# A four-layer trunk on one core: the small TensorE steps of an attention head, gathered in one place per head

## The chip, the cores and the metric

The kernel runs on one core of one Trainium2 chip. Its time is the device time of one execution in microseconds (us); three runs of the kernel before gave a median of 1296.69 us. Engines are named as in the profile: PE is TensorE, PEld its weight loads, DVE VectorE, ACT ScalarE, POOL GpSimd, SP SyncE. "L857" is line 857 of the kernel before. Behind the point where the diff takes away a line, the changed kernel's numbers are one lower; the lines that are named here are the same in both.

## The reference, cut to what matters

A trunk of four layers works on 256 tokens of 1024 channels. Each layer has a mixer, a feed-forward block and a gated side input, with two layer norms. Layers 0 and 3 mix by differential attention, layer 1 by a gated recurrence, layer 2 by local attention with a window of 128 tokens and a sink. The change touches the two kinds of attention:

```python
# differential attention (8 heads, each with two score maps)
s = einsum('bmqd,bmkd->bmqk', q, k);  s = where(rel >= 0, s + bias, -inf)
a = softmax(s);  a = a[:, :, 0] - lam_full * a[:, :, 1]
o = einsum('bhqk,bhkv->bhqv', a, v);  o = rms_norm(o, subln) * (1 - lam_init);  return o @ w_out

# local attention (16 query heads that share 2 key heads, with a sink)
m = maximum(max(s), sink);  e = exp(s - m);  a = e / (sum(e) + exp(sink - m))
o = einsum('bnhgqk,bnkhd->bnqhgd', a, v);  return o @ w_out
```

All is float32.

## The kernel before, in words

**Large matmuls.** Weights come from HBM as 1 MB chunks (SP issues them, in the order of use). ScalarE rounds each chunk to a high part `wh` (L124), VectorE subtracts it to get a low part `wl` (L125), and TensorE adds up three products: high by high, high by low, low by high. L177 to L179 are these three where tokens are the rows of the result (feed-forward, V, output projection); L197 and L198 are the same work where channels are the rows (Q and K projection, 16 matmuls per 128 columns), which ScalarE and VectorE then join from two halves (L204, L208).

**Small steps of a head.** In both kinds of attention a head goes through these steps, and "head" in local attention means a pair of query heads, 0 to 7, one for each key head:

- `soft`: scores on TensorE (L644 and L648; in local attention L816 and L818), bias and maximum on VectorE (L653; L821, then the small L830 and L831), exponentials on ScalarE (L661; L836 and, for the sink, L840), normalisation on VectorE (in local attention L841, L842 and the scaling L845 of `e`; in differential attention L673 subtracts the second map).
- `attT`: transposes of `e` on TensorE (three L684; in local attention six L857), copied by ScalarE to `aT` (L686; two L859).
- `pv`: P times V on TensorE (L694 to L696; L868 to L870). In local attention its result is split at once into `hT` (ScalarE L124, VectorE L125), the input of the output projection; in differential attention an RMS norm follows.
- `outT` (differential attention only): transposes of the normed output (L721), then the same split.

**Order.** Large matmuls are pushed to a queue as generators. `self.fill(us)` takes from it about as many as that many microseconds hold, and `self.fill_to(g)` all up to g. The program's text so says where the small steps stand between them. When the program is built, a scheduler sets each engine's order once: it may take an instruction of later text ahead where it counts the earlier one as not ready, if its inputs and its buffer are there. On the chip each engine then works through its own order and waits where an input is not ready.

**PSUM.** The program uses eight banks: four buffers of the tag `mm` (`self.mm_ps()`) and four of the tag `acc` (`self.acc_ps()`). Projections accumulate in `mm`; scores, PV and, before the change, the transposes of local attention use `acc`. Buffers are given in the order of the text.

**Around the change.** In differential attention the loop over 8 heads runs while the Q and K projections of later heads and the second half of V fill the queue. Before, one turn of the loop is: projections up to this head, 2.93 us of filler, `soft(hd)`, `attT(hd-1)`, 2.6 us of filler, `outT(hd-2)`, `pv(hd-1)`; the later heads' `pv` and `outT` stand behind the loop, among the output projection. In local attention a turn is: Q projection up to this head (every second turn), 1.3 us of filler, `soft(a)`, 3.25 us of filler, `pv(a-2)`, 0.65 us of filler, `attT(a-1)`. The Q projection holds less filler than the eight turns ask for. Behind the loop the first parts of the output projection are pushed (`out_part`), with `pv(6)`, `attT(7)` and `pv(7)` among them; each takes two `mm` buffers when it starts.

## Time and profile before

| | us |
|---|---|
| median of three runs (lowest to highest) | 1296.69 (1296.45 to 1298.39) |
| the profiled execution | 1296.76 |
| its span | 1294.8 |
| span, head 0's scores to head 3's scores in local attention | 21.27 (705.80 to 727.07) |
| span, head 3's scores to PV of head 6 | 18.40 (727.07 to 745.47) |

A row of the timeline gives the start in us from the span's beginning, how long the instruction took, the engine, the line, the operation, the tiles out<-in with the shape, and a count where rows of equal instructions are merged; brackets at the end give idle time of the engine just before, and what ended it. A matmul of scores or PV stands in the trace as two rows. Matmuls overlap in these times, the next starting before the one before has ended; so what a matmul costs is read from one start to the next. In a table by stretches the numbers are the stretch, its length, the busy time of PE, PEld, DVE, ACT and POOL, the granted clock of TensorE, the share of the DMA engines, and GB/s.

### The profile page before, as it was taken

To read this page: it belongs to the slowest core of one execution; us is meant where nothing else is said; L and a number is where in the kernel's file an instruction comes from. 1 tells how busy PE (TensorE), PEld (TensorE's weight loads), DVE (VectorE), ACT (ScalarE), POOL (GpSimd) and SP (SyncE) were. 2 spreads that over 40 slices of the span, in tenths; PEclk is the share of its full clock that TensorE was granted. 3 is DMA by queue.
4 is the path that set the end of the run, shared out by engine and by line. 5 is a ranking of instruction groups with operands and counts; after the bars stand their busy time and mean duration, and the time that the engine had idled before them with its cause. 6 is when DMAs were issued, how large, how long until landed. Compare 5 with 4: busy or idle time off the path is not lost.

```text
span 1294.8 us, 18557 instructions
## 1 busy us (share of the span) xinstructions
PE 1287.8 (99%) x7034; PEld 1087.3 (84%) x7034; DVE 937.3 (72%) x1741; ACT 692.0 (53%) x1296; POOL 35.9 (3%) x48
## 2 busy tenths in 40 slices
PE   9999999999999999999999999999999999999998
PEld 6888888888888888888888788888888888888887
DVE  5888766667889877666677796666687877766666
ACT  5885544444754455444537755444447775444443
POOL 0001000000000010000000000000000010000000
PEclk9999999999999999999999999999999999999999
DMA  8745655553733256555547145655538344655540
GB/s 274 289 171 195 230 193 195 184 189 122 267 127 131 77 211 225 185 190 194 195 166 264 66 166 221 202 191 195 195 131 298 131 171 163 234 191 194 195 162 33
DMA packets 43081, 240.09 MB, mean 185 GB/s; under 512 B 4512, under 2 KB 11744, under 8 KB 16496
## 3 DMA queue, kind: packets, MB, share of 16 engines
q1 hardware_dynamic: 42992, 238.91, 52.8%
q8 instruction: 55, 0.90, 0.3%
q14 instruction: 34, 0.28, 0.1%
HBM read 237.79 MB, written 1.10 MB: 184 GB/s over the span
## 4 chain that ended last, share of the span: by engine, by line
PE 99%; DMA 1%; ACT 0%; DVE 0%; SPq 0%; issue 0%
PE mm L197 24%; PE mm L198 12%; PE acc L177 9%; PE acc L178 9%; PE acc L179 9%; PE mm L177 9%; PE mm L179 9%; PE mm L178 9%; PE acc L1029 2%; PE mm L327 1%; PE mm L684 1%; PE acc L648 1%; PE acc L644 1%; DMA qk<-in_xT_dram 0%; PE acc L857 0%; DMA wr<-in_w_dram 0%
## 5 line engine op out<-in xcount | busy, mean ns | idle before, releaser
L125 DVE TENSOR_TENSOR wl<-wr,wh 128x1024 fp32r<-128x1024 f32 (+1 forms) x548 | 513.8, 967 | 158.4 <-ACT wh L124 157.8
L124 ACT ACTIVATE wh<-wr 128x1024 fp32r<-128x1024 f32 (+1 forms) x548 | 445.6, 852 | 219.4 <-PE acc L179 77.4
L197 PE MATMUL mm<-hT,wh 128*128 128x512 f32 x1344 | 481.6, 400 | 0.0
L198 PE MATMUL mm<-hT,wl 128*128 128x256 f32 x1344 | 377.9, 282 | 0.0
L197 PEld LDWEIGHTS mm<-hT,wh 128*128 128x128 f32 x1344 | 252.6, 188 | 60.0 <-issue 1.8
L198 PEld LDWEIGHTS mm<-hT,wl 128*128 128x128 f32 x1344 | 254.3, 189 | 2.9 <-DVE wl L125 0.4
L177 PE MATMUL acc<-wh,uh 128*128 128x512 f32 x512 | 201.0, 393 | 0.4 <-ACT uh L124 0.4
L178 PE MATMUL acc<-wl,uh 128*128 128x512 f32 x512 | 200.0, 391 | 0.0
L179 PE MATMUL acc<-wh,ul 128*128 128x512 f32 x512 | 199.7, 390 | 0.0
L177 PE MATMUL mm<-wh,hT 128*128 128x512 f32 (+1 forms) x536 | 197.1, 368 | 0.9 <-ACT wh L124 0.8
L178 PE MATMUL mm<-wl,hT 128*128 128x512 f32 (+1 forms) x536 | 193.2, 360 | 0.5 <-DVE wl L125 0.5
L179 PE MATMUL mm<-wh,hT 128*128 128x512 f32 (+1 forms) x536 | 192.8, 360 | 0.0
L204 ACT COPY cr<-mm 128x256 f32<-128x256 f32 x168 | 61.0, 363 | 117.0 <-PE mm L198 116.9
L177 PEld LDWEIGHTS mm<-wh,hT 128*128 128x128 f32 x536 | 101.5, 189 | 16.0 <-ACT wh L124 1.8
L177 PEld LDWEIGHTS acc<-wh,uh 128*128 128x128 f32 x512 | 96.1, 188 | 22.2 <-ACT uh L124 1.9
L179 PEld LDWEIGHTS mm<-wh,hT 128*128 128x128 f32 x536 | 101.3, 189 | 15.8 <-issue 1.0
L179 PEld LDWEIGHTS acc<-wh,ul 128*128 128x128 f32 x512 | 96.2, 188 | 21.1 <-DVE ul L125 0.8
L178 PEld LDWEIGHTS mm<-wl,hT 128*128 128x128 f32 x536 | 101.5, 189 | 14.6 <-DVE wl L125 1.2
L178 PEld LDWEIGHTS acc<-wl,uh 128*128 128x128 f32 x512 | 96.2, 188 | 17.9
L124 ACT ACTIVATE uh<-r 128x512 fp32r<-128x512 f32 x55 | 34.7, 631 | 101.5 <-DVE r L478 101.1
L208 DVE TENSOR_TENSOR r<-mm,cr 128x256 f32<-128x256 f32 x110 | 46.4, 421 | 28.3 <-ACT cr L204 23.0
L318 POOL TENSOR_TENSOR rs<-rp,mhalf 128x2 f32<-128x2 f32 (+2 forms) x36 | 33.1, 918 | 1123.1 <-DVE rp L317 1123.1
(167 smaller groups left out, 983.7 us busy)
## 6 DMA issues: line engine op xcount, KB each, us to landing
wr<-in_w_dram SPq DMA_DIRECT2D x207, 1024.0 KB, 4.9
lng<-in_ln_g_dram SPq DMA_DIRECT2D x8, 512.0 KB, 3.9
lnb<-in_ln_b_dram SPq DMA_DIRECT2D x8, 512.0 KB, 4.6
bt<-ud SPq DMA_DIRECT2D x2, 2048.0 KB, 10.4
wr<-in_w_dram SPq DMA_DIRECT2D x8, 256.0 KB, 5.8
bt<-ud SPq DMA_DIRECT2D x1, 1280.0 KB, 13.3
qk<-in_xT_dram SPq DMA_DIRECT2D x4, 256.0 KB, 5.9
h<-in_x_dram SPq DMA_DIRECT2D x2, 512.0 KB, 11.7
```

Source lines behind the costliest of these rows:

```text
L124: self.nc.scalar.activation(hi, src, AF.Copy),
L125: self.nc.vector.tensor_tensor(lo, src, hi.bitcast(F32), op=ALU.subtract),
L177: mm(out, l[0], r[0], start=start, stop=False)
L178: mm(out, l[0], r[1], start=False, stop=False)
L179: mm(out, l[1], r[0], start=False, stop=stop)
L197: mm(bank, wh, hT.both[:, kt].rearrange("p a t -> p (a t)"), start=kt == 0, stop=False)
L198: mm(bank[:, S:], wl, hT[0][:, kt, :], start=False, stop=kt == KT - 1)
L204: self.nc.scalar.copy(x, bank[:, S:])
L208: self.nc.vector.tensor_tensor(*views, op=ALU.add)
L318: nc.gpsimd.tensor_tensor(out, t, self.mhalf[:, :n], op=ALU.pow)
L327: nc.tensor.transpose(pt[:, j * P : j * P + P], src[:, c : c + P], self.ident)
L1029: nc.tensor.matmul(pl[lo:hi, o : o + w], KS[:, a, b * P + lo : b * P + hi], Qr[:, a, n0 : n0 + g, 1, :], start=True, stop=True,)
```

## The change

In differential attention, `outT` and `pv` move from behind the 2.6 us of filler to ahead of it, right behind `attT`, and take one head earlier: `outT(hd-3)` and `pv(hd-2)` instead of `outT(hd-2)` and `pv(hd-1)`. In local attention, `attT(a-1)` and `pv(a-2)` stand right behind `soft(a)`, and the filler behind them is one piece of 3.9 us instead of 3.25 and 0.65. The transposes of local attention take buffers of the tag `mm` instead of `acc`. The arithmetic is the same.

```diff
@@ differential attention, the loop over heads
                 soft(hd)
                 if hd > 0:
                     attT(hd - 1)
+                if 0 <= hd - 3 < 4:
+                    outT(hd - 3)
+                if 0 <= hd - 2 < 4:
+                    pv(hd - 2)
                 self.fill(2.6)
-                if 0 <= hd - 2 < 4:
-                    outT(hd - 2)
-                if 0 <= hd - 1 < 4:
-                    pv(hd - 1)
@@ local attention, attT
                 for g in range(2):
-                    pt = self.acc_ps()
+                    pt = self.mm_ps()
@@ local attention, the loop over heads
                 soft(a)
-                self.fill(3.25)
+                if a > 0:
+                    attT(a - 1)
                 if a > 1:
                     pv(a - 2)
-                self.fill(0.65)
-                if a > 0:
-                    attT(a - 1)
+                self.fill(3.9)
```

What this does to the engines' orders is shown at three places. In the names a number tells one buffer's use from another; it is not the same in both programs.

TensorE in the first layer, before: the second place of a head, between large matmuls of the projections.

```order
L197 MATMUL mm_673<-hT_72,wh_661 128x512
L198 MATMUL mm_673<-hT_72,wl_662 128x256
L721 MATMUL acc_576<-ident,o_581 128x128 x2
L694 MATMUL acc_686<-v_96,aT_646 128x128
L695 MATMUL acc_686<-v_96,aT_646 128x128
L696 MATMUL acc_686<-v_96,aT_646 128x128
L197 MATMUL mm_673<-hT_72,wh_667 128x512
```

And now, with the same steps behind the scores and transposes of a later head.

```order
L644 MATMUL acc_603<-qk_482 128x128
L648 MATMUL acc_602<-qk_482 128x256
L648 MATMUL acc_603<-qk_482 128x256
L684 MATMUL mm_623<-ident,e_493 128x128 x3
L721 MATMUL acc_523<-ident,o_528 128x128 x2
L694 MATMUL acc_633<-v_96,aT_521 128x128
L695 MATMUL acc_633<-v_96,aT_521 128x128
L696 MATMUL acc_633<-v_96,aT_521 128x128
L197 MATMUL mm_586<-hT_72,wh_559 128x512
```

The large matmuls ahead of L721 and those between it and L684 are now in one piece. Counted over the program, small steps stand between large matmuls in 132 places before and in 118 now: 4 fewer in the first layer, 5 fewer in the last, 5 fewer in local attention.

TensorE in local attention, before: from PV of head 2 to PV of head 3 (`mm_7213` and `mm_7214` are accumulators of the output projection, `e_6968` belongs to head 3, `q_6859` to head 5).

```order
L179 MATMUL mm_7213<-wh_7223,hT_6548 128x512
L857 MATMUL acc_7054<-ident,e_6968 128x128
L177 MATMUL mm_7214<-wh_7217,hT_6548 128x512
L857 MATMUL acc_7054<-ident,e_6968 128x128 x2
L857 MATMUL acc_7060<-ident,e_6968 128x128 x3
L816 MATMUL acc_7069<-kv_6549,q_6859 128x128
L816 MATMUL acc_7070<-kv_6549,q_6859 128x128
L818 MATMUL acc_7069<-kv_6549,q_6859 128x256
L818 MATMUL acc_7070<-kv_6549,q_6859 128x256
L868 MATMUL acc_7094<-aT_7058,v_6550 64x128
```

And now, the same heads (`q_6943` belongs to head 6).

```order
L816 MATMUL acc_7069<-kv_6549,q_6859 128x128
L818 MATMUL acc_7069<-kv_6549,q_6859 128x256
L816 MATMUL acc_7070<-kv_6549,q_6859 128x128
L818 MATMUL acc_7070<-kv_6549,q_6859 128x256
L857 MATMUL mm_7045<-ident,e_6968 128x128 x3
L857 MATMUL mm_7051<-ident,e_6968 128x128 x3
L868 MATMUL acc_7106<-aT_7049,v_6550 64x128
L869 MATMUL acc_7106<-aT_7049,v_6550 64x128
L870 MATMUL acc_7106<-aT_7049,v_6550 64x128
L868 MATMUL acc_7106<-aT_7055,v_6550 64x128
```

The transposes write `mm` buffers, and no large matmul is between the heads any more. From head 3's scores on, 18 large matmuls of the output projection stood between the small steps up to PV of head 6; now the first of them stands inside the transposes of head 6, and the other 17 behind it. In the built program the transposes of the last heads use all four `mm` banks in turn, and the two first accumulators of the output projection get the banks of head 5's transposes.

VectorE in local attention, before: the normalisation of head 4 (`sm_7019`, `e_7017`) ahead of the bias and maximum of head 5 (`e_7066`).

```order
L841 TENSOR_TENSOR sm_7019<-sm_7019,se_7032 128x4
L842 RECIPROCAL sm_7019<-sm_7019 128x4
L845 TENSOR_SCALAR e_7017<-e_7017,sm_7019 128x128
L845 TENSOR_SCALAR e_7017<-e_7017,sm_7019 128x256
L845 TENSOR_SCALAR e_7017<-e_7017,sm_7019 128x128
L845 TENSOR_SCALAR e_7017<-e_7017,sm_7019 128x256
L821 ISA e_7066,mx_7067<-acc_7069,bt_6551 128x128
```

And now, the normalisation of head 4 among the bias and maximum of head 6 (`e_7115`).

```order
L841 TENSOR_TENSOR sm_7019<-sm_7019,se_7032 128x4
L821 ISA e_7115,mx_7116<-acc_7119,bt_6551 128x128
L821 ISA mx_7116 128x1
L842 RECIPROCAL sm_7019<-sm_7019 128x4
L821 ISA e_7115,mx_7116<-acc_7119,bt_6551 128x256
L821 ISA mx_7116 128x1
L845 TENSOR_SCALAR e_7017<-e_7017,sm_7019 128x128
L845 TENSOR_SCALAR e_7017<-e_7017,sm_7019 128x256
```

VectorE now scales `e` of a head behind the scores of the second head after it.

## The prediction

> **What bounds the kernel now.** I read the page first: the span, the busy shares, and the engines' shares of the chain that ended last.

> ```profile
> span 1294.8 us, 18557 instructions
> PE 1287.8 (99%) x7034; PEld 1087.3 (84%) x7034; DVE 937.3 (72%) x1741; ACT 692.0 (53%) x1296; POOL 35.9 (3%) x48
> ...
> PE 99%; DMA 1%; ACT 0%; DVE 0%; SPq 0%; issue 0%
> ```

> TensorE is the chain, nearly everywhere. So only two things can move the time: what TensorE loses when it goes from the large matmuls to small ones and back, and new waits in its queue. Both are read from the distance between starts in the timeline, since the busy time is modelled and two matmuls overlap in it.

> **Price of a break, differential attention.** The PE timeline of the first layer, around the transposes of a head (L684) and the second place (L721, L694 to L696) that goes away:

> ```profile
> 61.73 0.55 PE L684 MATMUL mm<-ident,e 128*128 128x128 f32 x3
> 62.03 0.48 PE L197 MATMUL mm<-hT,wh 128*128 128x512 f32 x1
> 62.35 0.28 PE L198 MATMUL mm<-hT,wl 128*128 128x256 f32 x1
> 62.47 0.39 PE L197 MATMUL mm<-hT,wh 128*128 128x512 f32 x1
> 62.70 0.28 PE L198 MATMUL mm<-hT,wl 128*128 128x256 f32 x1
> ...
> 64.78 0.28 PE L198 MATMUL mm<-hT,wl 128*128 128x256 f32 x1
> 64.90 0.38 PE L721 MATMUL acc<-ident,o 128*128 128x128 f32 x2
> 65.11 0.39 PE L694 MATMUL acc<-v,aT 128*128 128x128 f32 x2
> ...
> 65.56 0.39 PE L696 MATMUL acc<-v,aT 128*128 128x128 f32 x2
> 65.70 0.48 PE L197 MATMUL mm<-hT,wh 128*128 128x512 f32 x1
> 66.02 0.28 PE L198 MATMUL mm<-hT,wl 128*128 128x256 f32 x1
> ```

> In the steady stream L197 to L198 takes 0.23 us (62.47 to 62.70) and L198 to the next L197 0.12 (62.35 to 62.47). Going in, L198 to L721 takes 0.12: nothing lost. Coming out, the first L197 holds TensorE for 0.32 (65.70 to 66.02, also 62.03 to 62.35), 0.09 too long; but the last small matmul before it gave way early. Two L721 take 0.21 (64.90 to 65.11), so a small matmul 0.105; yet three L684 take 0.30 (61.73 to 62.03) instead of 0.32, and L696's two 0.14 (65.56 to 65.70) instead of 0.21. So 0.02 to 0.07 of the 0.09 comes back, and a break costs 0.02 to 0.07. The change takes away 9 such breaks (4 in the first layer, 5 in the last), all of them behind L696 or L721: 0.2 to 0.6 us. I take 0.2, the price behind L696, which most of them have. No wait comes here: each moved step runs later than before, so its input is older, and its PSUM bank was freed a head before.

> [...]

> **Price of a break, local attention.** Here the PV matmuls (L868 to L870) are entered and left at another price:

> ```profile
> 724.22 0.28 PE L198 MATMUL mm<-hT,wl 128*128 128x256 f32 x1
> 724.43 0.43 PE L868 MATMUL acc<-aT,v 128*64 128x128 f32 x2
> ...
> 725.51 0.50 PE L197 MATMUL mm<-hT,wh 128*128 128x512 f32 x1
> 725.84 0.28 PE L198 MATMUL mm<-hT,wl 128*128 128x256 f32 x1
> ```

> In: 0.21 instead of 0.12. Out: 0.33 instead of 0.23. So up to 0.19. Five breaks go here, three of them beside transposes alone; I take 0.2 us for the five, within 0.05 and 0.95.

> **New waits, local attention.** The large matmuls of the Q projection run out before the fourth head (head 3). From there the kernel before still has filler: 18 matmuls of the output projection stand between the heads. In the changed program none does: the transposes now take tiles of the tag mm, the output projection's accumulators need the same four buffers, and in the code they come after the transposes of head 6. So from head 3's scores to head 6's transposes TensorE's queue holds small work only, while VectorE and ScalarE have the same work to do in less time. The stretch before, then the output projection's pace:

> ```profile
> 727.05:745.45 18.40, 18.40 (x149) 13.95 (x148) 14.83 (x85) 13.90 (x53) 0.00 (x0) 1.00 0.00 1
> ```
> ```profile
> 739.89 0.39 PE L177 MATMUL mm<-wh,hT 128*128 128x512 f32 x1
> ...
> 741.04 0.39 PE L179 MATMUL mm<-wh,hT 128*128 128x512 f32 x1
> ```

> The columns are the stretch, its length, the busy us of PE, PEld, DVE, ACT and POOL, and the granted clock (1.00): VectorE has 14.83 us of work in it. Five steps take 1.15, so a filler matmul is 0.23 and 18 of them 4.1 us. Durations and hand-overs for the chain, from the timelines of PE, DVE and ACT:

> ```profile
> 726.33 0.82 PE L857 MATMUL acc<-ident,e 128*128 128x128 f32 x6
> 727.07 0.49 PE L816 MATMUL acc<-kv,q 64*128 64x128 f32 x4
> ...
> 727.93 0.43 PE L868 MATMUL acc<-aT,v 128*64 128x128 f32 x2
> ...
> 729.00 0.88 PE L857 MATMUL acc<-ident,e 128*128 128x128 f32 x6
> ...
> 745.47 0.43 PE L868 MATMUL acc<-aT,v 128*64 128x128 f32 x2
> ```
> ```profile
> 722.24 0.17 DVE L831 TENSOR_SCALAR mx<-mx 128x4 f32<-128x4 f32 x1
> ...
> 724.44 0.16 DVE L841 TENSOR_TENSOR sm<-sm,se 128x4 f32<-128x4 f32 x1 [1.83 <-ACT se L840]
> ...
> 725.04 1.00 DVE L845 TENSOR_SCALAR e<-e,sm 128x128 f32<-128x128 f32 x4
> ...
> 728.03 0.29 DVE L821 CUSTOM_DVE_ANT_0 e<-acc,bt 128x128 f32<-128x128 f32 x1 [0.62 <-PE acc L818]
> ...
> 729.26 0.17 DVE L830 TENSOR_TENSOR mx<-mx,sk 128x4 f32<-128x4 f32 x1
> ```
> ```profile
> 722.44 0.40 ACT L836 ACTIVATE e<-e,mx 128x128 f32<-128x128 f32 x1 [1.26 <-DVE mx L831]
> ...
> 724.31 0.35 ACT L204 COPY cr<-mm 128x256 f32<-128x256 f32 x1
> ...
> 726.85 0.86 ACT L859 COPY aT<-acc 128x384 f32<-128x384 f32 x2
> ```
> ```profile
> 744.83 0.86 ACT L859 COPY aT<-acc 128x384 f32<-128x384 f32 x2
> ```

> On TensorE: transposes of a head 0.74 (726.33 to 727.07), scores 0.86 (to 727.93), PV 1.07 (to 729.00). Across: scores to bias and maximum (L821) 0.96, these 1.23; L831 to exponentials 0.20, these 1.87 (722.44 to 724.31); their end to L841 0.13, L841 to the scaling (L845) 0.2 to 0.6, that 1.00, its first half ready after 0.5; transposes to the copy 0.52, each half copy 0.43, and its end to PV 0.2 (744.83 + 0.43 to 745.47).

> Now the changed order, from the start of head 3's scores as 0, in the order in which DVE and ACT have it. Without waits: scores 3, transposes 2, PV 1, scores 4, PV 2 end at 4.6. Scores 5 need the bank of scores 4, whose last L821 stands behind head 3's L841, and so behind its exponentials (2.6 to 4.5): end at 5.65, 0.2 late. Transposes 3 need e of head 3: scaling from 5.6, half ready at 6.1, start 6.2 (wait 0.55), end 7.0. Their copy: 6.72 to 7.15; PV 3 at 7.35 (0.35) to 8.42; scores 6 to 9.28. Transposes 4: the exponentials of head 4 stand behind the copies of head 3 (7.58 to 9.45); head 4's L841 stands behind two L821 of head 6 (9.38 to 9.95), and the scaling behind the other two: 10.75; start 11.35, a wait of 2.07, the longest. They end at 12.15; PV 4 at 12.5, with transposes 5 woven in, to 14.3; scores 7 to 15.16. PV 5 needs the copy of head 5, which stands behind the exponentials of head 6 (13.6 to 15.47): 16.1 (0.95) to 17.2. Transposes 6 can start there. Without any wait they would start at 12.6: so the waits are 4.6 us.

> Then transposes 6, the 18 filler matmuls and two breaks: 17.2 + 0.75 + 4.1 + 0.2 = 22.3 to PV 6. Before it is 18.4 (727.07 to 745.47). So +3.9 us.

> One more wait: transposes of head 0 now stand one large matmul behind the scores of head 1.

> ```profile
> 705.80 0.49 PE L816 MATMUL acc<-kv,q 64*128 64x128 f32 x4
> ```
> ```profile
> 713.19 1.00 DVE L845 TENSOR_SCALAR e<-e,sm 128x128 f32<-128x128 f32 x4
> ```

> Scores of head 0 start at 705.80. They (0.86), 30 large matmuls at 0.35 a pair (5.3), the entry (0.1), scores 1 (0.86) and one large matmul (0.3) take TensorE to 713.2, while e of head 0 comes in quarters from 713.44 to 714.2, and no earlier than before, since all that makes it keeps its place. With six transposes of 0.105 behind the quarters, +0.3.

> **Sum.** −0.2 (differential) − 0.2 (breaks, local) + 3.9 + 0.3 = +3.8. The profiled execution took 1296.76 us, 1.96 more than its span and 0.07 more than the median of 1296.69. Forecast: 1296.76 + 3.8, 1300.6 us.

> Bounds. Below: VectorE never idle in that stretch. Two groups of its lines there are not the heads' work (behind the bar: busy us and mean ns):

> ```profile
> L125 DVE TENSOR_TENSOR wl<-wr,wh 128x512 fp32r<-128x512 f32 x1 | 0.7, 686 | 0.0
> L208 DVE TENSOR_TENSOR q<-mm,cr 128x256 f32<-128x256 f32 x1 | 0.4, 425 | 0.5 <-ACT cr L204 0.5
> ```

> Without them 13.7 us are left; 0.96 + 13.7 puts e of head 6 at 14.7, half of it at 14.2, so transposes 6 start 2.9 earlier than I have (14.3): 1297.7. Above: each of the five waits 0.3 longer than read, 1302.1, and no gain from the breaks, 1302.5.

> **Rivals.** (a) The breaks cost more than read, and nothing waits: TensorE gives back the dearest price, 0.19, at all 14 breaks: −2.7, 1294.1. Against it: the 0.12 into L721. For it: 0.21 into L868 and 0.33 out. It turns the sign if the breaks give back more than the waits cost, and shows in a measurement only if nearly no wait is left. [...] Chance 0.05.

> (b) VectorE and ScalarE keep up better than my chain, 0.7 us above the lower bound: 1298.4, no measurable change. For it: the order on both engines lets two heads overlap. It decides if transposes 4 wait under 0.8 instead of 2.07. Chance 0.18.

> (c) The clock falls in the stretch with waits. A 128x512 matmul at the program's start, before the clock is up, against 0.39 above:

> ```profile
> L264 PE MATMUL acc<-z 128*128 128x512 bf16 x10 | 4.3, 615 | 1.2 <-DVE z L261 1.2
> ```

> The 6 us of work after the waits at 615 instead of 390 ns would cost 3.5 more: 1304.2. Against it: the granted clock is 1.00 in the row of the stretch. Chance 0.05. [...]

> **How the numbers follow.** Forecast 0.72, (b) 0.18, (a) 0.05, (c) 0.05. The likeliest gives 1300.6. The range 1298.2 to 1302.6 takes in the bounds of the forecast but for the lowest 0.5 us, and about half of (b); left out are (a), (c) and the other half of (b). About 0.2%, 2.6 us, is what a measurement of this kernel can tell from no change, so slower begins at 1299.3: of the forecast's 0.72 some 0.05 lies below it; slower is 0.67 + 0.05 (c) + 0.02 of (b), 0.74; faster 0.05; the rest 0.21.

> **What would show it.** In the changed kernel's trace TensorE's distance between starts should be over 0.5 us ahead of L857 of head 4 and ahead of L868 of head 5, with releasers DVE L845 and ACT L859; from head 3's L816 to PV 6 22.3 us instead of 18.4; L177 to L179 of the output projection only behind head 6's transposes. The differential layers should keep their time per head. Wrong would be: local attention within 1 us of before, or a differential layer that gains over 0.5 us.

## The result and the profile after

The changed kernel takes 1303.97 us (median of 5 runs, 1303.75 to 1304.67) beside 1296.99 for the kernel before (5 runs, 1296.45 to 1298.39). The ratio is 1.0055, with a 95% interval from 1.0043 to 1.0066: it is 7.0 us slower. The forecast was 1300.6, 3.8 us slower, with 1302.6 as the upper end. The direction was right and the size was not.

The page of the changed kernel looks as it did before: TensorE is as busy in share, and only the span is longer.

```profile
span 1302.9 us, 18572 instructions
...
PE 1292.2 (99%) x7034; PEld 1088.4 (84%) x7034; DVE 935.7 (72%) x1741; ACT 692.6 (53%) x1296; POOL 36.0 (3%) x48
```

So the span is cut at places that both programs have: the first scores of an attention layer (L644, L816) and the first L327 behind its heads. The table by stretches of the kernel before, with the heads of the first layer, of local attention and of the last layer (the columns are those of the prediction, with the count of instructions in brackets, then the share of the DMA engines and GB/s):

```profile
29.51:117.90 88.39, 88.39 (x510) 73.06 (x509) 74.13 (x226) 65.25 (x187) 7.73 (x10) 1.00 0.63 228
...
705.80:765.00 59.20, 59.20 (x388) 47.12 (x388) 48.05 (x182) 42.16 (x126) 1.01 (x2) 1.00 0.32 113
...
993.78:1081.90 88.12, 88.12 (x510) 72.97 (x509) 70.65 (x219) 60.75 (x179) 6.97 (x10) 1.00 0.46 160
```

The same of the changed kernel:

```profile
30.41:119.30 88.89, 88.89 (x510) 73.25 (x510) 74.33 (x226) 65.26 (x187) 7.80 (x10) 1.00 0.62 226
...
707.15:772.70 65.55, 62.74 (x387) 48.71 (x387) 47.17 (x182) 42.47 (x126) 1.01 (x2) 0.97 0.29 100
...
1001.46:1089.93 88.47, 88.47 (x510) 72.97 (x510) 70.19 (x219) 60.76 (x179) 6.98 (x10) 1.00 0.46 161
```

Local attention loses 6.35 us (59.20 to 65.55) and the differential layers lose 0.50 and 0.35, where they should have gained 0.2 together. Everything between is the same to 0.1 us, but for the start: up to the first scores it is 29.51 us before and 30.41 after. That part differs from one execution to the next (29.80 us in e9, 30.08 in e2, 30.73 in e1; in e5 local attention starts at 709.85 us, 2.70 later than in the changed kernel, and the granted clock over the span is 0.997, where before has 1.000), and so the two spans differ by 8.1 us and the medians by 7.0.

TensorE in local attention, from head 3's scores (L816) to PV of head 6 (the last row):

```profile
728.77 0.49 PE L816 MATMUL acc<-kv,q 64*128 64x128 f32 x4
...
735.88 0.43 PE L868 MATMUL acc<-aT,v 128*64 128x128 f32 x2 [0.21 <-ACT aT L859]
...
739.61 1.16 PE L857 MATMUL mm<-ident,e 128*128 128x128 f32 x6 [1.62 <-DVE e L845]
740.93 0.43 PE L868 MATMUL acc<-aT,v 128*64 128x128 f32 x2 [0.17 <-ACT aT L859]
...
747.79 0.76 PE L857 MATMUL mm<-ident,e 128*128 128x128 f32 x4 [0.64 <-DVE e L845]
...
752.84 0.43 PE L868 MATMUL acc<-aT,v 128*64 128x128 f32 x2
```

The waits are there. The one ahead of head 4's transposes is where the prediction had it, with the releaser that it named (DVE L845); the other is ahead of head 6's transposes, also for DVE L845, and not ahead of PV of head 5. Head 4's transposes start 10.84 us behind head 3's scores (forecast 11.35). But PV 6 comes after 24.07 us, where 22.3 was forecast. What is new stands in the column of the granted clock, cut at the borders of its change:

```profile
735.09:738.50 3.41, 2.69 (x26) 1.83 (x23) 2.71 (x19) 3.15 (x14) 0.00 (x0) 1.00 0.02 5
738.50:741.91 3.41, 2.13 (x12) 1.36 (x13) 3.38 (x22) 2.60 (x10) 0.00 (x0) 1.00 0.00 0
741.91:745.33 3.42, 3.42 (x15) 2.44 (x16) 0.14 (x1) 2.90 (x12) 0.00 (x0) 0.50 0.00 0
```

For 3.41 us TensorE runs at 0.50. In the 3.41 us before that it started only 12 matmuls, with no idle time longer than 1.62 us, while VectorE was busy for 3.38.

### The profile page after: what moved, and what is told of

It reads as the page before. It is cut to its first block, busy times and chain, and to the rows that moved or that the text cites. A ratio compares the mean times of both kernels' runs of the same rounds, so it can differ in the third digit from the quotient of the medians.

```text
span 1302.9 us, 18572 instructions
## 1 busy us (share of the span) xinstructions
PE 1292.2 (99%) x7034; PEld 1088.4 (84%) x7034; DVE 935.7 (72%) x1741; ACT 692.6 (53%) x1296; POOL 36.0 (3%) x48
## 4 chain that ended last, share of the span: by engine, by line
PE 97%; DMA 1%; ACT 0%; DVE 0%; issue 0%; SPq 0%; ACTq 0%
PE mm L197 24%; PE mm L198 12%; PE acc L177 9%; PE acc L178 9%; PE acc L179 9%; PE mm L177 9%; PE mm L178 8%; PE mm L179 8%; PE acc L1028 2%; PE mm L327 1%; DMA wr<-in_w_dram 1%; PE mm L684 1%; PE acc L648 1%; PE acc L644 1%; DMA qk<-in_xT_dram 1%; PE mm L857 1%
## 5 line engine op out<-in xcount | busy, mean ns | idle before, releaser
L125 DVE TENSOR_TENSOR wl<-wr,wh 128x1024 fp32r<-128x1024 f32 (+1 forms) x548 | 513.8, 967 | 162.6 <-ACT wh L124 162.3
L197 PE MATMUL mm<-hT,wh 128*128 128x512 f32 x1344 | 480.4, 400 | 0.1
L198 PE MATMUL mm<-hT,wl 128*128 128x256 f32 x1344 | 377.8, 281 | 0.0
L197 PEld LDWEIGHTS mm<-hT,wh 128*128 128x128 f32 x1344 | 252.5, 188 | 60.9 <-issue 1.5
L198 PEld LDWEIGHTS mm<-hT,wl 128*128 128x128 f32 x1344 | 253.9, 189 | 2.9 <-DVE wl L125 0.4
L177 PE MATMUL acc<-wh,uh 128*128 128x512 f32 x512 | 200.8, 393 | 0.4 <-ACT uh L124 0.4
L179 PE MATMUL acc<-wh,ul 128*128 128x512 f32 x512 | 199.5, 390 | 0.0
L177 PE MATMUL mm<-wh,hT 128*128 128x512 f32 (+1 forms) x536 | 196.8, 367 | 1.5 <-ACT wh L124 0.8
L179 PE MATMUL mm<-wh,hT 128*128 128x512 f32 (+1 forms) x536 | 192.4, 359 | 0.0
L204 ACT COPY cr<-mm 128x256 f32<-128x256 f32 x168 | 61.2, 364 | 116.2 <-PE mm L198 116.1
L177 PEld LDWEIGHTS mm<-wh,hT 128*128 128x128 f32 x536 | 101.4, 189 | 16.7 <-ACT wh L124 1.8
L177 PEld LDWEIGHTS acc<-wh,uh 128*128 128x128 f32 x512 | 96.0, 188 | 22.3 <-ACT uh L124 1.9
L179 PEld LDWEIGHTS mm<-wh,hT 128*128 128x128 f32 x536 | 101.2, 189 | 15.6 <-issue 0.6
L179 PEld LDWEIGHTS acc<-wh,ul 128*128 128x128 f32 x512 | 96.1, 188 | 21.2 <-DVE ul L125 0.8
L208 DVE TENSOR_TENSOR r<-mm,cr 128x256 f32<-128x256 f32 x110 | 46.3, 421 | 28.9 <-ACT cr L204 23.5
## 6 DMA issues: line engine op xcount, KB each, us to landing
bt<-ud SPq DMA_DIRECT2D x1, 1280.0 KB, 13.6
```

The source lines that it names most:

```text
L125: self.nc.vector.tensor_tensor(lo, src, hi.bitcast(F32), op=ALU.subtract),
L177: mm(out, l[0], r[0], start=start, stop=False)
L179: mm(out, l[1], r[0], start=False, stop=stop)
L197: mm(bank, wh, hT.both[:, kt].rearrange("p a t -> p (a t)"), start=kt == 0, stop=False)
L198: mm(bank[:, S:], wl, hT[0][:, kt, :], start=False, stop=kt == KT - 1)
L204: self.nc.scalar.copy(x, bank[:, S:])
```

## The experiments

**One part of the change at a time.** e1 is the kernel before with the diff's first piece only (differential attention), e2 with the two others only (local attention). e3 and e4 take local attention's half apart: e3 has its last piece, the order, and e4 its second, the tag.

```diff
e1_da
+                if 0 <= hd - 3 < 4:
+                    outT(hd - 3)
+                if 0 <= hd - 2 < 4:
+                    pv(hd - 2)
                 self.fill(2.6)
-                if 0 <= hd - 2 < 4:
-                    outT(hd - 2)
-                if 0 <= hd - 1 < 4:
-                    pv(hd - 1)
e2_swa: e3 and e4 together
e3_order_only
-                self.fill(3.25)
+                if a > 0:
+                    attT(a - 1)
                 if a > 1:
                     pv(a - 2)
-                self.fill(0.65)
-                if a > 0:
-                    attT(a - 1)
+                self.fill(3.9)
e4_tag_only
-                    pt = self.acc_ps()
+                    pt = self.mm_ps()
```

> The kernel before with the change in differential attention alone; local attention is that of before. Theory A (a break is worth nothing here, since what is lost when the large matmuls are left and entered again comes back elsewhere; in the first layer the scheduler also splits head 2's scores): +0.3 to +0.9 us over before, of which +0.3 to +0.6 in the first layer and 0 to +0.4 in the last. Theory B (the prediction: 9 breaks at 0.02 to 0.07 us): -0.2 us, within -0.6 and 0.

> The kernel before with the change in local attention alone, order and tag. Theory A (waits of the small steps without filler, and one window of TensorE at half clock that follows them): +6.0 to +6.6 us, a stretch of 3.41 us at clock 0.5 between the transposes of head 4 and the scores of head 7, and 24 us from head 3's scores to PV 6. Theory B (the waits alone, the half clock being chance in one execution): about +4.2 us, clock 1.00 throughout, 22.3 us from head 3's scores to PV 6.

> The new order of the small steps in local attention, but their transposes in buffers of the tag acc as before. In the built program 28 large matmuls of the output projection then stand among the heads 3 to 5 again. Theory A (the tag took the filler away, and the waits come from that): within 1.0 us of before, clock 1.00 throughout. Theory B (gathering the steps makes each of them stand right behind what it needs, whatever lies between): +3 us or more.

> The order of before, only the transposes of local attention in buffers of the tag mm. In the built program no large matmul is left between the heads 2 to 6. Theory A (the tag took the filler away): +4 to +6.6 us, with waits of over 0.5 us ahead of the transposes or PV of heads 4 and 5, and perhaps a stretch at clock 0.5. Theory B (the gathered order makes the waits): within 0.5 us of before.

Measured against 1297.34 us before: e1 1297.77 (ratio 1.0005, 0.9996 to 1.0014), e2 1302.81 (1.0040, 1.0028 to 1.0052), e3 1299.51 (1.0018, 1.0010 to 1.0027), e4 1300.65 (1.0026, 1.0016 to 1.0037; 3.3 us, less than the 4 to 6.6 of its theory A). The times alone can't tell e1 from before; its stretches can: the first layer's heads, where their code is that of before, take 88.25 to 88.39 us in before, e2, e3 and e4, and the last layer's 88.11 or 88.12. First and last layer of e1, then first layer, local attention and last layer of e2:

```profile
30.73:119.45 88.72, 88.72 (x509) 73.17 (x509) 74.28 (x226) 65.26 (x187) 7.79 (x10) 1.00 0.63 228
...
995.38:1083.84 88.46, 88.46 (x509) 72.96 (x509) 70.07 (x219) 60.74 (x179) 6.98 (x10) 1.00 0.46 162
```
```profile
30.08:118.43 88.35, 88.35 (x509) 73.01 (x509) 74.13 (x226) 65.25 (x187) 7.72 (x10) 1.00 0.64 228
706.32:770.29 63.97, 61.17 (x388) 47.61 (x387) 48.08 (x184) 43.16 (x127) 1.01 (x2) 1.00 0.30 102
999.18:1087.30 88.12, 88.12 (x510) 72.90 (x510) 70.65 (x219) 60.79 (x179) 6.97 (x10) 1.00 0.46 160
```

The differential half costs 0.33 and 0.34 us a layer: theory A, and the prediction's gain is refuted. In e2 the same code of local attention takes 63.97 us at clock 1.00 throughout, 4.77 over before, where the changed kernel took 65.55. So in its profiled execution (1301.98) e2 goes by theory B in the clock and lies between the theories in time, while its five times spread from 1301.52 to 1303.10. Its TensorE:

```profile
727.87 0.49 PE L816 MATMUL acc<-kv,q 64*128 64x128 f32 x4
...
738.71 1.16 PE L857 MATMUL mm<-ident,e 128*128 128x128 f32 x6 [1.62 <-DVE e L845]
...
745.37 0.76 PE L857 MATMUL mm<-ident,e 128*128 128x128 f32 x4 [0.64 <-DVE e L845]
...
750.42 0.43 PE L868 MATMUL acc<-aT,v 128*64 128x128 f32 x2
```

The same two waits to 0.01 us, and from head 3's scores to PV 6 22.55 us: near the forecast's 22.3. The waits are a matter of the program; the half clock is not there in each execution, and is worth 65.55 − 63.97 = 1.6 us by these two.

The tag alone (e4) makes waits in the old order, too; local attention loses 3.9 us by it (63.09 against 59.20):

```profile
733.34 1.16 PE L857 MATMUL mm<-ident,e 128*128 128x128 f32 x6 [0.60 <-DVE e L845]
735.04 0.43 PE L868 MATMUL acc<-aT,v 128*64 128x128 f32 x2 [0.55 <-ACT aT L859]
743.02 0.43 PE L868 MATMUL acc<-aT,v 128*64 128x128 f32 x2 [0.44 <-ACT aT L859]
```

The new order alone (e3), with the large matmuls back between the heads, has no idle time of TensorE in local attention that the profile lists, and the clock is 1.00 there. So the waits go by theory A, but the time does not: e3 is 2.2 us slower, between the 1.0 of theory A and the 3 of theory B. Local attention takes 61.85 us, 0.93 of it for four more large matmuls ahead of the first L327. Half a microsecond of the rest shows in the distances between starts, 0.25 too long between two L177 and 0.27 ahead of head 0's transposes; the remainder is spread over many entries and is not settled. By their stretches, without those four matmuls, order and tag alone cost 1.7 and 3.9 us, and both together, in e2, 4.8: part of the one is in the other.

**The clock.** e5 is the changed kernel with four matmuls without use behind the scores of head 6; c_after is the changed kernel without an edit:

```diff
                 es[a] = e
+                if a == 6:
+                    for _ in range(4):
+                        nc.tensor.matmul(
+                            scs[1][:, 384:], self.ident, kv[:, 0, :P], start=True, stop=True
+                        )
```

> The changed kernel, with four matmuls that are of no use (0.215 us each, 0.86 us, into columns of a bank that nobody reads) behind the scores of head 6, so in the waits ahead of transposes and PV of head 4. Everything else stands as it was. Theory A (the clock was halved because one window of 3.41 us held under about 1 us of matmuls that are no transposes): no stretch at clock 0.5 inside local attention, the stretch from head 3's scores to PV 6 22.5 to 23.0 us instead of 24.07, and 1302.4 to 1302.9 us. Theory B (the half clock has nothing to do with how much TensorE does there): the stretch at 0.5 stays, and the extra matmuls make it 1304.2 to 1304.8 us.

> The changed kernel once more, beside the others of this call. Theory A: the windows of the clock run freely, so the stretch at 0.5 comes in some executions and not in others: two groups of times, about 1302.4 and 1304.0 us. Theory B (the half clock belongs to the program): all times within 0.5 us of 1304.

Measured: c_after 1303.67 us (1.0047, 1.0035 to 1.0060); its five times are 1302.51, 1302.54, 1303.67, 1303.86 and 1304.04. These are the two groups of theory A, some 1.3 us apart, and theory B falls. None of the traces is of the lower group; the start doesn't explain it, since the profiled execution (1304.04) has its first scores at 29.8 us, and 1302.5 would need 28.3, earlier than in any trace here. With the five of the result, all above 1303.7, 8 of 10 executions lie in the upper one. The profiled execution of c_after is of the upper group and shows the half clock at another place, 2.87 us behind the start of head 6's scores (736.77) and not 4.85 (737.06 in the changed kernel):

```profile
736.23:739.64 3.41, 1.79 (x19) 1.09 (x14) 2.72 (x19) 3.41 (x18) 0.00 (x0) 1.00 0.00 0
739.64:743.06 3.42, 3.42 (x14) 2.15 (x14) 2.10 (x12) 2.59 (x10) 0.00 (x0) 0.50 0.00 0
```

The half clock lasts 3.41 us in the changed kernel and 3.42 in c_after, and it lies at different places of the program. What decides that it comes in one execution and not in another is not shown. e5 has none in local attention, which takes 63.91 us there at 1.00, with 22.51 us from head 3's scores to PV 6; its median is 1302.96 (1.0042, 1.0029 to 1.0056). That agrees with theory A in the time, but it is weak: some executions of the changed kernel are as short (c_after's lower group), and the extra matmuls waited themselves for VectorE (1.42 us) and came later than meant. (The profiled execution of e5, 1305.79 us, is the one with the slow start.) A stretch of the same length in e5 and one in e2, which hold the wait behind head 6's scores or its end; neither is followed by a half clock:

```profile
739.45:742.87 3.42, 2.00 (x18) 1.42 (x17) 2.73 (x19) 3.34 (x17) 0.00 (x0) 1.00 0.00 0
```
```profile
738.03:741.44 3.41, 2.56 (x15) 1.61 (x16) 3.10 (x19) 2.56 (x11) 0.00 (x0) 1.00 0.00 0
```

The modelled busy time doesn't order the four stretches: 1.79 and 2.13 us ahead of the half clock, 2.00 and 2.56 in these two. An estimate from the rows counts each matmul that starts in a stretch at its distance in a dense stream: 0.107 us for each 128 columns of the small ones, and half of that for each of the two rows of a matmul in scores and PV. The 3.41 us ahead of the half clock then hold 1.02 us of work in the changed kernel and 1.07 in c_after. That so little work brings the half clock about is the author's reading of these two traces; no run shows it.

**Transposes and the clock.** The changed kernel with 68 transposes without use ahead of head 4's, in e6:

```diff
                     pt = self.mm_ps()
+                    if a == 4 and g == 0:
+                        for _ in range(68):
+                            nc.tensor.transpose(pt[:, :P], kv[:, 0, :P], self.ident)
```

and in its place in e7:

```diff
                     pt = self.mm_ps()
+                    if a == 4 and g == 0:
+                        for _ in range(34):
+                            nc.tensor.matmul(pt[:, :P], kv[:, 0, :P], self.ident, start=True, stop=True)
```

> The changed kernel with 68 transposes of no use (0.108 us each, 7.3 us in one piece) ahead of head 4's transposes: TensorE is busy, with transposes alone, for over two windows of the clock. Theory A (transposes don't count as work for the clock): the clock falls to 0.5 inside that piece or right behind it, for at least one window. Theory C (any matmul counts): the clock stays at 1.00 through the piece, since TensorE is never idle in it, and about 5.5 us are added.

> The same with 34 matmuls (0.215 us each, 7.3 us) in place of the 68 transposes. Both theories: the clock stays at 1.00 in the piece and behind it; the waits of head 4 are covered by it, so about 5.5 us are added to the 1302.4 that the changed kernel takes without a stretch at half clock. If the clock falls here as well, what counts is something else than the kind of matmul.

Measured: one execution each, 1306.78 and 1307.34 us. The stretch of e6 with the 68 transposes, and the one behind it; then those of e7:

```profile
734.69:742.12 7.43, 7.43 (x71) 7.43 (x70) 4.53 (x26) 4.41 (x20) 0.00 (x0) 1.00 0.01 2
742.12:746.00 3.88, 3.88 (x39) 3.04 (x39) 1.53 (x8) 1.81 (x5) 0.00 (x0) 1.00 0.00 0
```
```profile
735.02:742.61 7.59, 7.59 (x70) 7.59 (x69) 4.52 (x26) 4.39 (x20) 0.00 (x0) 1.00 0.01 2
```

The clock stays at 1.00 through 7.43 us of transposes alone. Theory A falls, theory C stands: in e6 the clock stayed up on transposes as it did on the matmuls of e7 (1.00 through 7.59 us). Both kernels add less than forecast, since the piece covers more waits than that of head 4: local attention takes 68.30 and 68.40 us, 4.3 and 4.4 over e2's 63.97.

**What bounds the stretch with waits.** e10 is the changed kernel without the scaling of the exponentials, which leaves the division by the row sums out of the softmax:

```diff
-                for g in range(2):
-                    for b, s in enumerate(spans):
-                        nc.vector.tensor_scalar(
-                            e[:, g, s], e[:, g, s], sm[:, b, g : g + 1], None, op0=ALU.mult
-                        )
```

> The changed kernel without the scaling of the exponentials by the row sums in local attention (L845), which leaves that part of the softmax out: 1.00 us of VectorE less for each head, and one hand-over less between the exponentials and the transposes. Theory A (the waits are the chain of VectorE and ScalarE, whose work has nothing between it any more): the wait ahead of head 4's transposes goes from 1.62 to under 0.5 us, from head 3's scores to PV 6 20 to 21.5 us instead of 22.5, no stretch at clock 0.5, 1299.5 to 1301.5 us. Theory B (the waits are the banks of the tag mm, or the order on TensorE): the stretch stays at 22 us or more.

Measured: 1300.98 us (1.0031, 1.0019 to 1.0043), no half clock. From head 3's scores to PV 6, and the transposes of head 4 among PV of head 3 (L852 and L863 are the lines L857 and L868, shifted):

```profile
727.68:749.13 21.45, 21.13 (x149) 14.27 (x148) 16.15 (x79) 17.50 (x65) 0.00 (x0) 1.00 0.10 30
```
```profile
734.55 0.33 PE L852 MATMUL mm<-ident,e 128*128 128x128 f32 x1
735.04 0.44 PE L852 MATMUL mm<-ident,e 128*128 128x128 f32 x2 [0.16 <-ACT e L836]
735.40 0.43 PE L863 MATMUL acc<-aT,v 128*64 128x128 f32 x2
735.77 0.33 PE L852 MATMUL mm<-ident,e 128*128 128x128 f32 x1
736.02 0.43 PE L864 MATMUL acc<-aT,v 128*64 128x128 f32 x2
```

Within theory A's numbers, at their upper ends: the wait of 1.62 us is gone, what is left is released by ScalarE, and the stretch is 1.1 us shorter than in e2. It isn't shorter by more, for two reasons. ScalarE is now the busy one (17.50 of 21.45 us). And transposes woven into PV cost extra here: one transpose takes 0.25 to the next PV row (735.77 to 736.02), instead of 0.109 between two of the 68 transposes of e6 (7.43 us).

**The differential layers.** e9 is the kernel before with its second place split in two. e8 is the changed kernel with PV ahead of `outT`, and e11 the changed kernel with one more transpose behind the three of a head:

```diff
e9_more_breaks
-                self.fill(2.6)
+                self.fill(1.3)
                 if 0 <= hd - 2 < 4:
                     outT(hd - 2)
+                self.fill(1.3)
                 if 0 <= hd - 1 < 4:
                     pv(hd - 1)
e8_pv_first
-                if 0 <= hd - 3 < 4:
-                    outT(hd - 3)
                 if 0 <= hd - 2 < 4:
                     pv(hd - 2)
+                if 0 <= hd - 3 < 4:
+                    outT(hd - 3)
e11_extra_transpose
                     nc.tensor.transpose(pt[:, s], e[:, 0, s], self.ident)
+                nc.tensor.transpose(pt[:, 384:], e[:, 0, :P], self.ident)
```

> The kernel before with 1.3 of the 2.6 us of filler of each turn put between the transposes of the normed output and PV in differential attention: 6 places more in the program where small steps stand between large matmuls (138 instead of 132). Theory A (a break is worth 0.00 us here): each differential layer within 0.1 us of before (88.39 and 88.12), but for stretches that change their pace. Theory B (the prediction's price, 0.02 to 0.07): +0.06 to +0.2 a layer. [...]

> The changed kernel with PV ahead of the transposes of the normed output in differential attention, so that a gathered place ends with those transposes and no longer with PV; nothing else is changed. Theory A (a gathered place costs nothing by itself; what the differential layers lose is the pace of the large matmuls behind it, 353.3 ns a pair instead of 347, which depends on how TensorE comes out of the place): the last layer's heads take 88.46 us again if the stretches behind the places run at 353 ns, and 88.0 to 88.1 if they run at 347; the time of a layer follows the pace, 0.107 us for each stretch of 17 pairs. Theory B (gathering itself costs, whatever the pace): 88.46 with stretches at 347.

> The changed kernel with a fourth transpose of 0.108 us, of no use, behind the three of each head in differential attention, so that TensorE comes to the large matmuls behind a gathered place 0.108 us later against its own rhythm. 8 of them add 0.86 us to a layer if the paces stay. Theory A (the pace behind a place, 347 or 353.3 ns a pair, hangs on the moment at which TensorE comes out of it): at least one of the four slow stretches of the last layer runs at 347, and its heads take 0.11 us less for each, 88.9 to 89.2 us. Theory B (a long piece of large matmuls behind a gathered place is always at 353): all four at 353, 89.3 us.

e9 takes 1297.09 us against 1297.03 (1.0001, 0.9992 to 1.0010), its layers 88.29 and 88.15 us against 88.39 and 88.12: six breaks more, three a layer, cost nothing that shows. The last layer is the clean one, since all its large matmuls keep their pace: 0.03 us for three breaks, 0.01 each. (In the first layer the paces of the large matmuls changed as well, by about −0.1 us in sum.) Theory A; the prediction's 0.02 to 0.07 and its dearest price, 0.19, fall for the places with PV and transposes.

What the last layer loses instead is seen in the starts of the high-part matmuls (L197) of one long piece. The changed kernel in the last layer, second and last L197 behind a gathered place, 15 pairs apart; then the kernel before, 7 pairs apart:

```profile
1018.02 0.40 PE L197 MATMUL mm<-hT,wh 128*128 128x512 f32 x1
...
1023.33 0.40 PE L197 MATMUL mm<-hT,wh 128*128 128x512 f32 x1
```
```profile
1014.03 0.40 PE L197 MATMUL mm<-hT,wh 128*128 128x512 f32 x1
...
1016.46 0.39 PE L197 MATMUL mm<-hT,wh 128*128 128x512 f32 x1
```

That is 0.354 and 0.347 us a pair. The same stream has two paces, and in the last layer of both kernels a piece keeps one of them from its start to its end. Before, only the first piece of the last layer runs at 353 ns; in the changed kernel four more do, of 17 pairs, so 16 distances, each: 4 × 16 × 0.0063 = 0.40 us, enough for the 0.35 that the layer loses. In e8 (1304.09 us; 1.0058, 1.0045 to 1.0071) the four are at 353 again and the layer takes 88.46, so it tells nothing between its theories. e11 (one execution, 1306.79 us) moves TensorE by one transpose, and one of the four goes to the fast pace, 15 pairs in 5.21 us:

```profile
1027.39 0.40 PE L197 MATMUL mm<-hT,wh 128*128 128x512 f32 x1
...
1032.60 0.39 PE L197 MATMUL mm<-hT,wh 128*128 128x512 f32 x1
```

So the pace is no property of a long piece behind a gathered place; with one transpose more in each place ahead, one of the four left it. The time of e11 missed both theories: 89.59 us for the layer, 1.12 more than the changed kernel's 88.47 and not 0.86. (The granted clock over its span is 0.997, where the changed kernel has 0.998.) What sets the pace is not settled.

The first layer loses its 0.50 us otherwise: there the changed kernel has fewer pairs at the slow pace than before (50 against 68), but one place more than the text asks for. The scheduler took head 2's first score ahead; the PE timeline there, then the same pairs before:

```profile
44.12 0.28 PE L198 MATMUL mm<-hT,wl 128*128 128x256 f32 x1
44.34 0.48 PE L644 MATMUL acc<-qk 64*128 64x128 f32 x2
44.75 0.39 PE L198 MATMUL mm<-hT,wl 128*128 128x256 f32 x1
44.97 0.39 PE L197 MATMUL mm<-hT,wh 128*128 128x512 f32 x1
45.20 0.28 PE L198 MATMUL mm<-hT,wl 128*128 128x256 f32 x1
45.41 0.37 PE L644 MATMUL acc<-qk 64*128 64x128 f32 x1
...
46.26 0.55 PE L684 MATMUL mm<-ident,e 128*128 128x128 f32 x3
```
```profile
43.90 0.40 PE L198 MATMUL mm<-hT,wl 128*128 128x256 f32 x2
44.14 0.40 PE L197 MATMUL mm<-hT,wh 128*128 128x512 f32 x1
```

From the first of two L198 to the next L197 it is 0.85 us with the score between them (44.12 to 44.97) and 0.24 before. The rest of the scores takes no less for it: from the last L198 to L684 1.06 us (45.20 to 46.26), and 1.07 before. So the split costs 0.6 us, more than the layer loses. e11 agrees: there the scheduler leaves head 2's scores together, and its eight extra transposes add only 0.56 us to the changed kernel's first layer, where they add 1.12 to the last.

## Why the prediction was right in direction and wrong in size

- **The filler is gone and the waits come: right.** Shown by e4 (the tag alone makes waits) and e3 (no idle time listed with the filler back). Head 0's scores to head 3's scores: +0.35 in the changed kernel, forecast +0.3. Head 3's scores to PV 6 at full clock: 22.55 us in e2, forecast 22.3.
- **The chain inside it: right at its ends, not in the middle.** Head 4's wait was put at 2.07 and is 1.62. No wait of over 0.5 us comes ahead of PV 5 (forecast 0.95); transposes 6 wait instead (0.64, for VectorE). And weaving transposes 5 into PV 4 was costed at nothing, where e10's rows show 0.14 for such a change. So the total is near in part because errors offset each other.
- **The clock holds: the step that failed.** Its fall cost 1.6 us in the profiled execution, a term that the sum has at nothing, and it alone puts the time outside the range: without the 1.6 us it would be 1302.4, about where c_after's lower group lies (1302.51 and 1302.54). The ground for it, the granted clock of 1.00 in the row of the stretch, was read from the kernel before, with the filler in it. Rival (c) had the fall at a chance of 0.05, and its time, 1304.2 (its terms add up to 1304.1), is near the result by luck: its price of 3.5 us was twice too high (3.41 us at half clock, not 6 us of work), and other terms made up for it. The longest wait doesn't tell it either: 1.62 us in the changed kernel and in c_after, with the half clock behind it, and 1.62 in e2 at 1.00. Transposes alone kept the clock at 1.00 in e6, for 7.43 us.
- **Breaks at 0.02 to 0.07 us in differential attention: wrong.** They are worth 0.01 (e9's last layer). The term was −0.2 and the layers measured +0.50 and +0.35: in the first the scores that the scheduler split (0.6), in the last the pace of the large matmuls (0.4). "No wait comes here" held.
- **Breaks at −0.2 in local attention: counted twice.** Four of the five places that go lie between head 3's scores and PV 6 (6 before, 2 after), and the 18.4 and 22.3 us of that stretch hold them already.
- **Behind PV 6: a term that was missing.** From there to L327 it is 19.53 us before and 19.86 after. One row takes 0.41 too long, which is more than the difference: an accumulator of the output projection stands in the bank of head 7's transposes and its first matmul waits for their copy; the two L177 take 0.87 to the next row, where two in a stream take 0.46:

```profile
755.40 0.82 PE L857 MATMUL mm<-ident,e 128*128 128x128 f32 x6
755.98 1.04 PE L177 MATMUL mm<-wh,hT 128*128 128x512 f32 x2
756.85 0.39 PE L178 MATMUL mm<-wl,hT 128*128 128x512 f32 x1
```

The sum by the profiles: waits and what lies behind PV 6, 4.77 (e2, forecast 4.0 with its breaks); half clock 1.6 (forecast 0); differential layers 0.85 (forecast −0.2). Together 7.2, against 7.0 between the medians.

## What to carry to other kernels

Before moving a small step to another PSUM tag, look who else takes that tag's banks next: the matmuls that covered the waits could no longer start, and that was the larger part of the loss. Where TensorE will have waits, read the granted clock behind them in more than one execution, and don't go by the longest wait or by the clock of the kernel before: here it was 0.50 for 3.41 us behind a wait of 1.62 us, and 1.00 behind the same wait in e2, whose local attention is the same. Places where transposes and PV interrupt large matmuls of the projections cost 0.01 us each here; measure their price before paying for their removal. And see what the scheduler makes of the new order: scores that it split cost 0.6 us.
